# Last phase of a one-core encoder layer: where z's sigmoid is written, when gates are opened and rows finished, and the order of the last unit

## The chip, the cores and the metric

The kernel runs as one program on one core of a Trainium2 chip. The metric is the device time of one execution in microseconds, the median of several runs. The profile is of one execution, taken by the hardware profiler. Engines are named as in the profile: PE (matmul), PEld (weight load), DVE (vector), ACT (scalar, activations), POOL (GpSimd) and SP (the queue from which nearly all DMAs are issued, in order).

## The reference

One layer over 2048 prompt rows (16 tiles of 128) and 8 running streams of 16 rows each (one tile of 128, "the sample", tile number NT = 16). After an adaLN norm, `h @ w_in` gives for each row the q, k, v and z of two branches and the merge gates ga and gb. Both attentions run, the sample's also over caches of 512 past positions. What the last phase computes is:

```python
oa = rms_norm(oa, subln_g) * (1.0 - lam_init)
ya = (oa.reshape(b, s, WIDTH_A) * jax.nn.silu(za)) @ w_branch_a
yb = (ob.reshape(b, s, WIDTH_B) * jax.nn.silu(zb)) @ w_branch_b
out = (jax.nn.sigmoid(ga) * ya + jax.nn.sigmoid(gb) * yb) @ w_out
xp = xp + gate * out            # then y = rms_norm(xp, final_g)
```

All inputs and outputs are float32. The kernel splits each float32 operand of a large matmul into two float16 parts and adds three products.

## The kernel before

**Units.** The projection and the attention go by units: 8 units, each one head (A, even units) or one pair of heads (B, odd units). `steps` lists (unit, tile); within a unit the sample's tile NT stands first, then tiles 0 to 15. For each step the projection (`project`, L423 for q, k, v and z, L495 for a share of the merge gates) is cut into pieces, and all pieces of all steps stand in one list, `line`. The transposes of a step's q and k (`transpose_qk`) stand in the line after piece 5 of the next step. The main loop (L1330) runs over n: for each step it takes from the line up to a target that is paced by the estimated durations and runs LEAD = 5 steps ahead, and interleaves these pieces with the scores of step n and the products of weights and values (`pv`, L706 and L707) of step n - 2. When the line is empty, `early_work` fills the remaining steps evenly: the last branch weight, `first` of tiles 0 and 1 (their inputs), and four branch pieces and a transpose of tile 0. z, o and the gates go through DRAM (z_d, o_d, g_d), the sample's q, k and v through s_d.

**Last phase.** It goes over `tiles` = 0 to 14, the sample, 15, in steps n of its own. For each tile:

- `inputs` loads o (L1218, into hs[0]), z (L1219, into hs[1]) and the gates (L1223, four buffers, two a tile). It takes z's sigmoid into a PSUM bank of tag `mm`, of which there are two, shared with the branch matmuls. POOL multiplies o by z (L1230), DVE multiplies by the sigmoid (four L1236 for half 0, one L1232 for half 1). Then ACT takes the gates' sigmoids in place, then the sum of squares of o, and ACT and DVE (L287, L292) split o into u16, which lies in hs[2].
- `turned` transposes u16 by DMA (L1251).
- `branches`: 48 matmuls in four groups (L1262), each times a gate on DVE (L1264); POOL adds the two branches (L1266); `finish` sums squares (L274), scales and splits the result into y16.
- `turned_y` transposes it by DMA (L1287) into the only buffer of y^T.
- `output`: 48 matmuls (L1399) in two halves, times gate and scale (L1403), plus x on POOL (L1407). Then the row's sum of squares, its rsqrt on DVE (`rsqrt_one`, L255 to L266), the scaling (L1412) and the store (L1413). x has two buffers (L1392).

In step n the branches of tile n run, the output of tile n - 1 and the inputs of tile n + 2. Beside them runs the sample's attention over the caches in pieces (`sample`): cache loads (L758), key transposes (L777) copied out by DVE or ACT (L778), scores (L794), sigmoids or exponentials on ACT, a scan on DVE (L607), transposes of the weights (L812, L818), products (L830).

**Order.** A planner at build time gives each engine its order, by program order and by when its model says that operands are there; on the chip every engine runs its own list in order. Activations that need a table (sigmoid, exponential) go through a helper that keeps them in program order:

```python
def act(**kw):
    i = S.activation(**kw)
    if last_table[0] is not None:
        tc.add_manual_dep(i.ins, last_table[0].ins.name, NOSYNC, reason="table order")
    last_table[0] = i
    return i
```

Their line in the profile is L120, whatever they work on.

Of the kernel before, what the change touches and what calls it, by code (L numbers as in the profile page):

```python
# [16 lines left out]
F32 = mybir.dt.float32  # L17
# [3 lines left out]
AF = mybir.ActivationFunctionType  # L21
ALU = mybir.AluOpType
# [3 lines left out]
P = 128  # L26
D = 1024
# [5 lines left out]
NT = SEQ // P  # L33
# [77 lines left out]
def layer_kernel(ctx: ExitStack, tc: tile.TileContext, a: dict):  # L111
    nc = tc.nc
    V, S, G, T = nc.vector, nc.scalar, nc.gpsimd, nc.tensor
# [4 lines left out]
# [7 lines that stand above are left out]
# [30 lines left out]
    def y_rows(t):  # L155
        return y_p[t * P : (t + 1) * P, :] if t < NT else y_s
# [30 lines left out]
    def bank(tag, dt=F32):  # L187
        return ps.tile([P, 512 if dt == F32 else 1024], dt, tag=tag, name=f"ps_{tag}", bufs=BANKS[tag])
# [113 lines left out]
    units = [None] * 8  # L302
# [200 lines left out]
    def transpose_qk(U, t):  # L503
        g, i = t // 4, t % 4
        q16, k16 = U.pop(("q16", t)), U.pop(("k16", t))
        pt = bank("t", F16)
        for c in range(2):
            T.transpose(pt[:, c * P : (c + 1) * P], k16[:, c, :, :].rearrange("p f d -> p (f d)"), id16)
        for f in range(2):
            for c in range(2):  # L510
                j = 2 + f * 2 + c
                T.transpose(pt[:, j * P : (j + 1) * P], q16[:, f, c, :, :].rearrange("p r d -> p (r d)"), id16)
        if i == 0:
            U["k"][g] = kvp.tile([P, 2, 512], F16, tag="k", name="k", bufs=K_BUFS)
        U["q", t] = qst = stg.tile([P, 4, P], F16, tag="qst", name="qst", bufs=Q_BUFS)
        kst = U["k"][g][:, :, i * P : (i + 1) * P]
        copy = V.tensor_copy if U["kind"] == 1 else S.copy
        (V.tensor_copy if U["u"] == 0 else copy)(out=kst, in_=pt[:, 0:256].rearrange("p (c n) -> p c n", c=2))
        copy(out=qst, in_=pt[:, 256:768].rearrange("p (j n) -> p j n", j=4))
# [343 lines left out]

        return [lambda x=x: one(*x) for x in srcs]

    steps = [(u, t) for u in range(8) for t in [NT] + list(range(NT))]
    back = []
    spare = norms()
    jobs, done = [], []
# [1 line left out]

    line = []

    def begin(u, t):
        if t == NT:
            if u > 0:
                free.extend(units[u - 1]["bufs"])
            finish_unit(u)

    def projection(m):  # L880
        u, t = steps[m]
        made = []

        def piece(i):
            if i == 0:
                begin(u, t)
                made.extend(project(units[u], t))
            if i == H_AT and not at_hand and m + 1 < len(steps) and steps[m + 1] not in ahead:
                fetch_h(*steps[m + 1])
            made[i]()  # L890

        return [lambda i=i: piece(i) for i in range(12 + 3 * GATES[u][1] // 128)]

    starts = []
    for m in range(len(steps)):
        starts.append(len(line))
        for i, fn in enumerate(projection(m)):
            line.append((m, fn))
            if i == TR_AFTER and m > 0 and steps[m - 1][1] < NT:
                line.append((m - 1, lambda m=m: transpose_qk(units[steps[m - 1][0]], steps[m - 1][1])))  # L900
    line.append((len(steps) - 1, lambda: transpose_qk(units[7], NT - 1)))
    starts.append(len(line))
    at = [0]

# [310 lines left out]
    def inputs(t):  # L1215

        o, z = hs[0:2]
        load(out=o, in_=o_d[t])  # L1218
        load(out=z, in_=z_d[t])  # L1219
        gs = []  # L1220
        for j in range(2):
            gs.append(L["g"][(2 * len(begun) + j) % 4].rearrange("p (b n) -> p b n", b=2))
            load(out=gs[j], in_=g_d[t].rearrange("p (b n) -> p b n", b=2)[:, :, j * 512 : (j + 1) * 512])  # L1223
        begun.append(t)
        r = L["orms"][:, 4 * t : 4 * t + 4] if t < NT else rsqrt(osums[:, NT, :], 4, P, tiny, "rA")
        for n in range(2):
            c = slice(n * 512, (n + 1) * 512)
            sg = bank("mm")
            act(out=sg, in_=z[:, c], func=AF.Sigmoid)
            G.tensor_tensor(out=o[:, c], in0=o[:, c], in1=z[:, c], op=ALU.mult)  # L1230
            if n == 1:
                V.tensor_tensor(out=o[:, c], in0=o[:, c], in1=sg, op=ALU.mult)  # L1232
            else:
                for h in range(4):
                    c = slice(h * P, (h + 1) * P)
                    V.scalar_tensor_tensor(out=o[:, c], in0=sg[:, c], scalar=r[:, h : h + 1], in1=o[:, c], op0=ALU.mult, op1=ALU.mult)  # L1236
        for g in gs:
            act(out=g, in_=g, func=AF.Sigmoid)
        acc = tiny.tile([P, 1], F32, tag="uacc", name="uacc")
        sum_squares(o, D, acc)  # L1240
        su = scales(acc, unit, "su")
        u16 = hs[2].bitcast(F16).rearrange("p (f n) -> p f n", f=2)
        split(u16[:, 0, :], u16[:, 1, :], o, su[:, 0:1], S)
        iu = unit.tile([P, 1], F32, tag="iu", name="iu")
        V.tensor_tensor(out=iu, in0=su[:, 1:2], in1=L["s"][0][:, 1:2], op=ALU.mult)
        return dict(u16=u16, u=L["u"][len(begun) % 2], iu=iu, g=gs)

    def turned(st):

# [56 lines left out]
    def early_work():  # L1306


        free.extend(units[7]["bufs"])

        def first(t):
            if "orms" not in L:
                L["orms"] = rsqrt(osums[:, 0:NT, :].rearrange("p t h -> p (t h)"), 4 * NT, P, con, "orms")
            states[t] = inputs(t)
            if t == tiles[0]:
                turned(states[t])

        def early(i):

            if i == 0:  # L1320
                L["first"] = [fn for _, fn in branches(states[tiles[0]])] + [lambda: turned_y(states[tiles[0]])]
            L["first"][i]()

        def rest():
            L["g"], L["u"], (L["y"], L["y16"]) = free[0:4], free[4:6], free[6:8]

        return [branch_weight for _ in branch_weights] + [rest] + [lambda t=t: first(t) for t in tiles[0:2]] \
            + [lambda i=i: early(i) for i in range(5)]
# [31 lines left out]
    with ExitStack() as c2:  # L1360
# [17 lines left out]
        def gate_rows(i, n):  # L1378
# [4 lines left out]
            T.matmul(pg, sel[0:9, i * P : (i + 1) * P], gsm[0:9, :], start=True, stop=True)  # L1383
            return pg

        def output(t, st):
            box = {}

            def half(j):
                if j == 0:  # L1390
                    box["x"] = s2.tile([P, D], F32, tag="x", name="x2", bufs=2)
                    load(out=box["x"], in_=x_rows(t))  # L1392
                x = box["x"]
                c = slice(j * 512, (j + 1) * 512)
                po = bank("o")
                n = 0
                for yi, wi in ((0, 0), (0, 1), (1, 0)):
                    for k in range(KT):
                        T.matmul(po, st["y"][:, yi * 8 + k, :], wo[j * 4 + k // 2][:, wi, k % 2, :], start=(n == 0), stop=(n == 3 * KT - 1))  # L1399
                        n += 1  # L1400
                m = s2.tile([P, 512], F32, tag="sg", name="m", bufs=2)
                if t < NT:
                    V.scalar_tensor_tensor(out=m, in0=po, scalar=st["iy"], in1=gate[:, c], op0=ALU.mult, op1=ALU.mult)  # L1403
                else:
                    S.activation(out=m, in_=po, func=AF.Identity, scale=st["iy"])
                    V.tensor_tensor(out=m, in0=m, in1=gate_rows(1, j), op=ALU.mult)
                G.tensor_tensor(out=x[:, c], in0=m, in1=x[:, c], op=ALU.add)  # L1407
                if j == 1:
                    acc = tiny.tile([P, 1], F32, tag="facc", name="facc")
                    sum_squares(x, D, acc)  # L1410
                    r = rsqrt_one(acc, D, tiny, "rF")
                    V.scalar_tensor_tensor(out=x, in0=x, scalar=r, in1=fg, op0=ALU.mult, op1=ALU.mult)  # L1412
                    load(out=y_rows(t), in_=x)  # L1413

            return [(5.2, lambda j=j: half(j)) for j in range(2)]

# [22 lines left out]
        for n in range(NT + 2):  # L1439
            work = []  # L1440
            if 0 < n <= NT:
                work += branches(states[tiles[n]])
            if n + 1 <= NT:

                work.insert(2, (0.9, lambda n=n: turned(states[tiles[n + 1]])))
            if n + 2 <= NT:
                work.insert(5, (0.1, lambda n=n: states.update({tiles[n + 2]: inputs(tiles[n + 2])})))
            if n > 0:
                work += output(tiles[n - 1], states.pop(tiles[n - 1]))
            if 0 < n <= NT:  # L1450
                work.append((0.9, lambda n=n: turned_y(states[tiles[n]])))
            interleave(work, aside(n))


# [25 lines left out]
```

## Time and profile before

| | |
|---|---|
| median of 3 runs | 2286.06 us (2282.44 to 2286.41) |
| the profiled execution | 2285.48 us, span 2283.7 us |
| busy, PE / PEld / DVE / ACT / POOL | 91% / 49% / 71% / 65% / 30% of the span |
| mean granted PE clock | 0.966 |
| DMA | 411.92 MB, mean 180 GB/s |

Busy time is the time in which an engine executes something. PE's matmuls are pipelined and their ends are modelled, so two that overlap count once. "A <- B" in the lists of waits says that A's engine stood idle until B was done. L numbers are lines of the kernel; a helper's line stands for every caller, and then the names of the tiles tell them apart (`wa<-g_d`: buffer wa, loaded from g_d). The buffers wa and wb are shared by weights, gates, u and y, and keep their names.

### The profile page before, as it was taken

To read this page: it belongs to the slowest core of one execution; us is meant where nothing else is said; L and a number is where in the kernel's file an instruction comes from. 1 tells how busy PE (TensorE), PEld (TensorE's weight loads), DVE (VectorE), ACT (ScalarE), POOL (GpSimd) and SP (SyncE) were. 2 spreads that over 40 slices of the span, in tenths; PEclk is the share of its full clock that TensorE was granted. 3 is DMA by queue.
4 is the path that set the end of the run, shared out by engine and by line. 5 is a ranking of instruction groups with operands and counts; after the bars stand their busy time and mean duration, and the time that the engine had idled before them with its cause. 6 is when DMAs were issued, how large, how long until landed. Compare 5 with 4: busy or idle time off the path is not lost. (4 is left out here: it accounts for less than half of the span.)

```text
span 2283.7 us, 40470 instructions
## 1 busy us (share of the span) xinstructions
PE 2085.1 (91%) x14478; PEld 1110.4 (49%) x14478; DVE 1611.5 (71%) x3507; ACT 1482.6 (65%) x2952; POOL 688.1 (30%) x559
## 2 busy tenths in 40 slices
PE   4997999999999999899999989999986799888997
PEld 2554554555555455455545555555543444444443
DVE  4668767789875778987577898776777656565554
ACT  3877677787876777786677777666776544444431
POOL 1522012355301335530032553012344232232321
PEclk7999999999999999999999999999997899999998
DMA  8667658697875778876566886757687989788652
GB/s 295 211 212 187 163 131 220 148 221 155 206 169 124 170 154 199 177 179 131 128 172 142 204 183 154 153 140 163 151 179 173 295 228 262 202 220 211 188 150 65
DMA packets 763754, 411.92 MB, mean 180 GB/s; under 512 B 524986, under 2 KB 708586, under 8 KB 763040
## 3 DMA queue, kind: packets, MB, share of 16 engines
q1 hardware_dynamic: 762474, 408.86, 72.6%
q8 instruction: 113, 1.85, 0.3%
q14 instruction: 89, 0.73, 0.1%
q10 hardware_dynamic: 1078, 0.48, 0.1%
HBM read 211.53 MB, written 72.91 MB: 125 GB/s over the span
## 5 line engine op out<-in xcount | busy, mean ns | idle before, releaser
L423 PE MATMUL ps_mm<-wb,hs 128*128 128x512 f16 x1836 | 460.7, 382 | 0.6 <-DVE v L292 0.5
L629 POOL TENSOR_TENSOR sc_p<-sc_p,sc_n 128x1024 f32<-128x1024 f32 (+8 forms) x160 | 278.1, 1742 | 459.2 <-DVE sc_n L607 451.6
L423 PEld LDWEIGHTS <-hs 128*128 128x128 f16 x2928 | 256.1, 98 | 226.9 <-issue 6.8
L607 DVE TENSOR_TENSOR_SCAN sc_n<-ps_s,sc_n,zero_t 128x512 f32<-128x512 f32 x192 | 245.3, 1278 | 64.4 <-ACT ps_s L120 62.2
L423 PE MATMUL ps_mm<-wa,hs 128*128 128x512 f16 x1092 | 279.4, 380 | 0.0
L647 PE MATMUL ps_s<-k,qst 128*128 128x512 f16 (+3 forms) x640 | 225.9, 354 | 38.3 <-DVE sc_n L607 30.1
L120 ACT ACTIVATE sc_p<-ps_s,usc 128x512 f32<-128x512 f32 (+3 forms) x320 | 202.0, 631 | 85.8 <-PE ps_s L648 55.1
L495 PE MATMUL ps_mm<-wa,hs 128*128 128x512 f16 x1020 | 257.0, 379 | 0.0
L562 DVE TENSOR_TENSOR sc_n<-sc_p,sc_n 128x1024 f16<-128x1024 f32 (+7 forms) x160 | 197.9, 1242 | 41.3 <-ACT sc_n L561 41.2
L648 PE MATMUL ps_s<-k,qst 128*128 128x512 f16 (+3 forms) x640 | 226.2, 354 | 0.0
L1399 PE MATMUL ps_o<-wo,wb 128*128 128x512 f16 x816 | 199.5, 401 | 24.7 <-DMA wb<-wa 22.0
L706 PE MATMUL ps_o<-v,wt 128*128 128x128 f16 x1008 | 175.6, 226 | 27.6 <-DMA wt<-sc_n 27.5
L495 PEld LDWEIGHTS <-hs 128*128 128x128 f16 x1632 | 140.2, 98 | 119.0
L120 ACT ACTIVATE ps_s<-ps_s,usc 128x512 f32<-128x512 f32 (+3 forms) x320 | 193.7, 605 | 0.0
L561 ACT CAST sc_n<-sc_p 128x1024 f16<-128x1024 f32 (+7 forms) x160 | 138.5, 870 | 49.2 <-POOL sc_p L629 49.1
L707 PE MATMUL ps_o<-v,wt 128*128 128x64 f16 x1008 | 158.5, 198 | 0.0
L495 PE MATMUL ps_mm<-wb,hs 128*128 128x512 f16 x612 | 155.9, 379 | 0.0
L706 PEld LDWEIGHTS <-wt 128*128 128x128 f16 x1008 | 99.2, 102 | 102.7 <-DMA wt<-sc_n 38.0
L1399 PEld LDWEIGHTS <-wb 128*128 128x128 f16 x816 | 82.1, 102 | 130.4 <-DMA wb<-wa 26.1
L457 POOL TENSOR_TENSOR rot<-pr,rope 128x256 f32<-128x256 f32 x68 | 63.1, 928 | 247.1 <-ACT pr L437 193.3
L437 ACT ACTIVATE pr<-ps_mm,usc 128x512 f32<-128x512 f32 (+1 forms) x136 | 86.5, 636 | 67.4 <-PE ps_mm L423 67.1
L545 DVE TENSOR_SCALAR_CACHE_REDUCE sc_n<-ps_s,usc 128x512 f32<-128x512 f32 (+3 forms) x148 | 99.0, 669 | 42.4 <-PE ps_s L648 28.2
(336 smaller groups left out, 4346.7 us busy)
## 6 DMA issues: line engine op xcount, KB each, us to landing
hs<-hT_d SPq DMA_DIRECT2D x122, 512.0 KB, 4.2
g_d<-gt SPq DMA_DIRECT2D x68, 256.0 KB, 3.4
out_dram<-pr SPq DMA_DIRECT2D x204, 64.0 KB, 1.8
wa<-g_d SPq DMA_DIRECT2D x25, 512.0 KB, 6.7
wide<-in_w_ada_dram SPq DMA_DIRECT2D x12, 1024.0 KB, 8.4
wa<-in_w_in_dram SPq DMA_DIRECT2D x44, 256.0 KB, 4.7
z_d<-pr SPq DMA_DIRECT2D x136, 64.0 KB, 2.7
o_d<-o SPq DMA_DIRECT2D x136, 64.0 KB, 2.7
```

The costliest lines, as they stand in the source:

```text
L120: i = S.activation(**kw)
L423: T.matmul(box["p"], box["h"][:, hi, k, :], U["w"][k][:, wi, :], start=(n == 0), stop=(n == 3 * KT - 1))
L495: T.matmul(box["g"][:, 0:gw], box["h"][:, hi, k, :], U["wg"][k // per][:, k % per, wi, :], start=(j == 0), stop=(j == 3 * KT - 1))
L561: S.copy(out=hi, in_=src)
L562: V.tensor_tensor(out=lo, in0=src, in1=hi, op=ALU.subtract)
L607: V.tensor_tensor_scan(out=dst[:, lo : lo + n][:, ::-1], data0=src[:, 0:n][:, ::-1], data1=zero_t[:, 0:1].to_broadcast([P, n]), initial=fi ...
L629: G.tensor_tensor(out=p[:, 0:m], in0=p[:, 0:m], in1=n[:, 1 : m + 1], op=ALU.mult)
L647: T.matmul(p[:, 0:n], qst[:, c, :], kk[:, c, 0:n], start=True, stop=False)
L648: T.matmul(p[:, 0:n], qst[:, 2 + c, :], kk[:, c, 0:n], start=False, stop=not diag)
L706: T.matmul(po[:, c * P : (c + 1) * P], wt[:, wj, :], vt[:, c, :, :], start=first, stop=False)
L707: T.matmul(po[:, c * P : c * P + 64], wt[:, nb + wj, :], vt[:, c, 0, :], start=False, stop=last)
L1399: T.matmul(po, st["y"][:, yi * 8 + k, :], wo[j * 4 + k // 2][:, wi, k % 2, :], start=(n == 0), stop=(n == 3 * KT - 1))
```

## The change

There are four parts, all in the last unit and the last phase.

1. z's sigmoid is written into hs[2], u's buffer, and read from there by L1236 and L1232. Before, it went to a PSUM bank.
2. The gates' sigmoids leave `inputs` for a function of their own, `opened`. In the last phase it is called one step after the loads; for tiles 0 and 1 it still follows their inputs.
3. The end of a row (sum of squares, rsqrt, scaling, store) leaves `output`: the row is put on the list `late`, and `finished` works it off in the next step, after that step's first two branch groups and the transpose of u. One call after the loop does the last row.
4. In unit 7 the sample's tile stands last in `steps`. `begin` looks whether the unit has been begun, in place of asking for tile NT, and the extra transposes after the end of the line go away, since the sample's pieces now follow tile 15.

```diff
-    steps = [(u, t) for u in range(8) for t in [NT] + list(range(NT))]
+    steps = [(u, t) for u in range(7) for t in [NT] + list(range(NT))] + [(7, t) for t in range(NT + 1)]
...
-    def begin(u, t):
-        if t == NT:
+    def begin(u):
+        if "sc" not in units[u]:
...
-    line.append((len(steps) - 1, lambda: transpose_qk(units[7], NT - 1)))
...
-            sg = bank("mm")
+            sg = hs[2][:, c]
             act(out=sg, in_=z[:, c], func=AF.Sigmoid)
...
-                    V.scalar_tensor_tensor(out=o[:, c], in0=sg[:, c], scalar=r[:, h : h + 1], in1=o[:, c], op0=ALU.mult, op1=ALU.mult)
-        for g in gs:
-            act(out=g, in_=g, func=AF.Sigmoid)
+                    V.scalar_tensor_tensor(out=o[:, c], in0=hs[2][:, c], scalar=r[:, h : h + 1], in1=o[:, c], op0=ALU.mult, op1=ALU.mult)
...
+    def opened(st):
+
+        for g in st["g"]:
+            act(out=g, in_=g, func=AF.Sigmoid)
...
             states[t] = inputs(t)
+            opened(states[t])
...
+        late = []
+
+        def finished():
+
+            while late:
+                x, t = late.pop(0)
+                acc = tiny.tile([P, 1], F32, tag="facc", name="facc")
+                sum_squares(x, D, acc)
+                r = rsqrt_one(acc, D, tiny, "rF")
+                V.scalar_tensor_tensor(out=x, in0=x, scalar=r, in1=fg, op0=ALU.mult, op1=ALU.mult)
+                load(out=y_rows(t), in_=x)
...
                 if j == 1:
-                    acc = tiny.tile([P, 1], F32, tag="facc", name="facc")
-                    sum_squares(x, D, acc)
-                    r = rsqrt_one(acc, D, tiny, "rF")
-                    V.scalar_tensor_tensor(out=x, in0=x, scalar=r, in1=fg, op0=ALU.mult, op1=ALU.mult)
-                    load(out=y_rows(t), in_=x)
+                    late.append((x, t))
...
                 work.insert(5, (0.1, lambda n=n: states.update({tiles[n + 2]: inputs(tiles[n + 2])})))
+                if n > 0:
+                    work.insert(6, (0.1, lambda n=n: opened(states[tiles[n + 1]])))
+            elif n + 1 <= NT:
+                work.insert(4, (0.1, lambda n=n: opened(states[tiles[n + 1]])))
+            work.insert(3, (0.1, finished))
...
+        finished()
```

More of the change, by code (lines that the diff above doesn't have):

```diff
@@ L885, in piece @@
             if i == 0:
-                begin(u, t)
+                begin(u)
                 made.extend(project(units[u], t))
```

## The prediction

> **What bounds the kernel now.** I read the busy time by stretches first, because the diff touches only the end of the attention and the last phase. Columns: stretch, length, then busy time (and instructions) of PE, PEld, DVE, ACT and POOL, granted clock, DMA share, GB/s. Below it are the last projection matmuls (L495), the last product of weights and values (L707), the first output matmul (L1399), and one branch group of 24 matmuls from the chain of waits.
>
> ```profile
> span 2283.7 us, 40470 instructions
> ...
> 1600.00:1690.00 90.00, 89.89 (x622) 47.29 (x620) 65.50 (x100) 65.71 (x126) 28.88 (x21) 1.00 0.65 153
> 1690.00:1764.00 74.00, 44.85 (x359) 25.91 (x358) 60.90 (x78) 50.71 (x80) 36.84 (x20) 0.75 0.86 185
> ...
> 1760.00:2080.00 320.00, 284.61 (x2080) 149.34 (x2079) 187.44 (x486) 144.76 (x268) 92.70 (x71) 0.94 0.90 241
> 2080.00:2284.00 204.00, 172.79 (x976) 79.91 (x974) 104.32 (x288) 67.18 (x124) 54.61 (x42) 0.94 0.53 142
> ...
> L495 PE MATMUL ps_mm<-wb,hs x612: 376/379/381, 640.4 to 1687.5; 128*128 128x512 f16 x153
> ...
> L707 PE MATMUL ps_o<-v,wt x1008: 191/193/261, 351.1 to 1763.1; 128*128 128x64 f16 x168
> ...
> L1399 PE MATMUL ps_o<-wo,wb x816: 376/379/635, 1790.6 to 2272.8; 128*128 128x512 f16 x164
> ...
> 2241.38 5.18 PE ps_mm L1262 x24
> ```
>
> Until 1690 PE is full (89.89 of 90 us): there PE's own work is the time. From the last projection (1687.5) to 1763 DVE leads (60.90 of 74) and PE starves. In the last phase PE leads, with the DMA engines close behind until 2080 (0.90). A matmul takes a slot of 5.18/24 = 0.216 us. So what the change can win there is PE's waiting. Next, then, who waits for whom from 1750 to the end: what waits, for what, total us, times, longest; PE, ACT, DVE and the load queue (SPq).
>
> ```profile
> PE ps_o L1399 <- DMA wb<-wa: 22.0, 9, 6.1
> PE ps_t L818 <- DVE dks L778: 9.7, 2, 4.9
> PE ps_s L777 <- DVE dsc L607: 6.8, 3, 2.9
> ...
> PE ps_mm L1262 <- DVE wa L1264: 2.9, 3, 2.1
> ...
> PE ps_t L763 <- DVE rF L266: 2.2, 1, 2.2
> ...
> PE ps_mm L1262 <- DVE r L256: 0.6, 1, 0.6
> ...
> ACT wa L120 <- DMA wa<-g_d: 51.6, 21, 7.0
> ...
> ACT wb L120 <- DMA wb<-g_d: 32.6, 8, 10.0
> ...
> DVE r L255 <- ACT junk L274: 40.1, 13, 5.9
> DVE dsc L607 <- ACT ps_s L120: 27.5, 6, 11.5
> ...
> SPq L1413 <- DVE x L1412: 65.2, 11, 18.5
> SPq L1392 <- DMA out_dram<-x: 36.7, 13, 6.2
> ...
> SPq L1287 <- PE ps_mm L1262: 21.1, 7, 5.7
> ```
>
> ACT stands 51.6 + 32.6 = 84.2 us with a gate's sigmoid at its head whose load has not landed. DVE stands 40.1 us with a row's rsqrt at its head. SP stands 65.2 us with a row's store at its head, and 36.7 us more because the next x load wants that store's buffer. PE itself shows far less: 9.7, 6.8, 2.9, 2.2, 0.6, and 22.0 for the transpose of y. I therefore price each part by the PE waits that it can reach, not by the idle time of the other engines.
>
> **Part 1, gates opened a step later.** No instruction is added or removed: two sigmoids a tile change their place on ACT. The functions that go through `act` keep program order, so a sample's sigmoids queue behind the gates'. The chain of waits at one such place:
>
> ```profile
> 2032.53 5.32 DMA wa<-g_d
> ...
> 2037.93 1.06 ACT wa L120
> ...
> 2039.32 0.51 ACT dsc L120
> 2039.84 0.50 ACT ps_s L120
> ...
> 2040.36 1.29 DVE dsc L607
> ...
> 2041.70 0.66 PE ps_s L777 x4
> ```
>
> Load, gate, the sample's sigmoids, DVE's scan, and only then PE's next transposes (L777). A step later the load has long landed, and the wait is gone. What PE gets is the L777 row: 6.8 us. I take -7. Bounds: 0 if the next thing is late anyway, and -16 if all three places return the 5.32 us of this load (3 x 5.32). Late next is PE's own matmul stream.
>
> **Part 2, z's sigmoid in u's buffer.** Two ACTIVATEs of 512 columns a tile write SBUF instead of two `mm` banks; the four L1236 and one L1232 on DVE read it there. The trace at one of the two long L818 waits, by POOL, ACT, DVE, PE:
>
> ```profile
> 2087.12 2.50 POOL L1230 TENSOR_TENSOR hs<-hs,hs 128x512 f32<-128x512 f32 x2 [12.04 <-DMA hs<-o_d]
> ...
> 2092.91 0.60 ACT L120 ACTIVATE ps_mm<-hs 128x512 f32<-128x512 f32 x1
> ...
> 2093.60 1.13 DVE L1236 SCALAR_TENSOR_TENSOR hs<-ps_mm,orms,hs 128x128 f32<-128x128 f32 x4 [8.03 <-ACT ps_mm L120]
> ...
> 2096.79 0.68 DVE L778 COPY dks<-ps_t 128x512 f32<-128x512 f32 x1
> ...
> 2097.52 0.47 PE L818 MATMUL ps_t<-ident,dsc 128*128 128x128 f32 x1 [4.90 <-DVE dks L778]
> ```
>
> DVE idles 8.03 us at L1236, the copy L778 that PE wants is behind it, and the sigmoid comes last although z was there. With u's buffer free (the transpose L1251 of the tile before has read it) the sigmoid no longer waits for a bank, and L1236 can start when POOL's product is done: 2087.12 + 2.50 = 2089.62 in place of 2093.60, 4.0 us. Twice that is -8; the bank waits (2.9 us) I leave out, since PE must wait for L1264 with two banks anyway. Bounds: 0 (the sigmoid keeps its late place on ACT) and -12.6 (9.7 + 2.9).
>
> What it adds are reads: L1236 and L1232 now have both inputs in SBUF. No row shows them so. The nearest is L562, which has two SBUF inputs, without and with a POOL instruction beside it:
>
> ```profile
> 1717.89 1.08 DVE L562 TENSOR_TENSOR sc_n<-sc_p,sc_n 128x896 f16<-128x896 f32 x1
> ...
> 1725.13 2.34 DVE L562 TENSOR_TENSOR sc_n<-sc_p,sc_n 128x896 f16<-128x896 f32 x1
> ...
> 1724.53 2.00 POOL L629 TENSOR_TENSOR sc_p<-sc_p,sc_n 128x1024 f32<-128x1024 f32 x1 [3.94 <-DVE sc_n L607]
> ```
>
> The second started inside POOL's 2.00 us and took 1.26 us more. One such meeting for each of 17 tiles is 17 x 1.26 = 21.4 us of DVE, not of PE: DVE is busy 104 to 187 us of these stretches, so idle time covers it, and I take 0. Bounds: 0 to +21.4. The Trainium skill, page "SBUF — State Buffer", section "SBUF: two separate sides", speaks against this edit: a DVE instruction with two SBUF inputs and a GpSimd one that reads SBUF lock a shared port pair for a whole instruction each, and the other blocks. The two L562 rows agree. By the page, with every meeting on the path, the sum below would end at 2289.
>
> **Part 3, rows finished a step later.** Square sum, rsqrt chain (ten small DVE instructions), scaling and store of a row move one step on. The squares are then ready when DVE comes to them, and SP meets the store when its row is done. PE's rows that name this chain are 2.2 (L266) and 0.6 (L256): -3. The 22.0 us for y's transpose (L1287) I leave: it waits for y^T's only buffer and for PE (21.1 us in SP's row). Bounds: 0 to -22. An x buffer is held a step longer; its load still comes a step ahead of the add that needs it. The last row's chain stays after the last matmul (2272.8), so the tail keeps its length.
>
> **Part 4, sample projected last in unit 7.** 48 matmuls (10.4 us of PE), two evictions on ACT, and on SP one load and six stores go from the head of the unit to the end of its line. But the line is paced: its last piece still falls at tile 13, where PE is full, so no PE work enters the starved stretch. Working through the loop by hand, the early work of the last phase moves half a step back against the attention: `first(0)` from tile 14 to tile 15, the four branch pieces from beside the last two products to the last and behind. That takes ACT and DVE work off tile 14 (a gain of some us) and may put 10.4 us of branch matmuls behind 1763. PE is free until the first L1399 at 1790.6, which covers 10.4 us. I take 0, bounds -4 to +10.4. SP's six stores fall among the transposes, where two more than before cost little.
>
> **Sum.** -7 - 8 - 3 + 0 = -18 us. The profiled execution took 2285.48 us (span 2283.7 and 1.8 around it), 0.6 below the median 2286.06. 2285.5 - 18 = 2267.5, so 2268.
>
> **Rivals.**
> - *More comes back.* The waits for y^T shrink too, as SP no longer stands behind row stores (65.2 + 36.7 us). Half of 22.0 more, and the bounds of parts 1 and 2: -16 - 12.6 - 3 - 11 = -43, 2243. Against it: SP's own row for L1287 names PE. At half of this extra, 2255.
> - *DMA is the bound.* At 0.90 until 2080, the loads may only move forward into a full queue: 2284, no change. Against it: 0.90 leaves 32 us of 320, and the share falls to 0.53 afterwards.
> - *Port.* Part 2's meetings on the path: 2267.5 + 21.4 = 2289, no change. Against it: DVE's idle time.
> - *A wait takes the place of the one removed (slower).* The sigmoid of z now waits for L1251, and what lies behind it on ACT is the second square sum of y, on which y^T and L1399 hang:
>
> ```profile
> 2162.21 4.05 SPq L1251 DMA_TRANSPOSE wb<-hs  x1
> ...
> 2176.30 0.63 ACT L274 ACTIVATE junk<-wa 128x512 f16<-128x512 f32 x1 [7.84 <-POOL wa L1266]
> ...
> 2176.93 0.58 ACT L120 ACTIVATE ps_mm<-hs 128x512 f32<-128x512 f32 x1
> ...
> DMA to landing us min/median/max: 4.3/6.8/8.5
> ```
>
> The last row is L1251's time to landing. Here it lands near 2169, 8 us ahead of the sigmoid: room. If the planner, seeing no bank in the way, puts the sigmoid right behind the split of u, ACT stands up to 6.8 us for each of 15 tiles, with y's sums behind. From 18/15 = 1.2 us a tile on y's path this decides; at 2 us it is 30 - 18 = +12: 2298.
>
> **How the numbers follow.** Forecast (2256 to 2279, with part 4's 10.4 at its upper end) 0.52, more 0.14, DMA 0.12, port 0.04, slower 0.18. A measurement of this kernel can tell about 0.2% (4.6 us) from no change, that is outside 2281.5 to 2290.6. Faster 0.52 + 0.14 = 0.66, same 0.16, slower 0.18. The range 2250 to 2293 leaves out the far parts of "more" (0.07) and of "slower" (0.11), under 0.2.
>
> **What would show it.** ACT's wait for g_d near zero, DVE's at L255 and SP's at L1413 mostly gone; L1236 starting right after POOL's L1230; the L818 and L777 waits of PE gone, L1399's near 22; attention's end within 5 us of 1763. Wrong if ACT waits for L1251 instead, if L1399's first start moves beyond 1800, or if the four L1236 grow from 1.13 us.

## The result and the profile after

The changed kernel takes 2297.62 us (median, 2293.24 to 2303.49), the kernel before 2286.41 us beside it. The ratio is 1.0052, with a 95% interval of 1.0038 to 1.0065: 11 to 12 us slower, where 18 us faster were forecast, and 4.6 us above the upper end of the range. The profiled execution took 2300.52 us.

Lines move a little: in the changed kernel the u transpose is L1253, the branch matmul L1264, POOL's product of o and z L1229, the four 128-column products L1235, the y transpose L1289, the output matmul L1414, the row's scaling and store L1398 and L1399.

First the busy time by stretches, in the columns of before.

```profile
1690.00:1764.00 74.00, 48.05 (x374) 26.97 (x372) 63.27 (x76) 52.85 (x84) 35.85 (x18) 0.75 0.80 168
1760.00:2080.00 320.00, 273.87 (x1912) 141.88 (x1910) 203.50 (x468) 140.91 (x264) 93.16 (x72) 0.91 0.87 231
2080.00:2299.00 219.00, 190.23 (x1140) 88.21 (x1139) 120.85 (x309) 71.92 (x132) 56.10 (x44) 0.95 0.59 152
```

Then the first and last start of the last projection, of the products of weights and values, and of the output matmuls (behind the colon the shortest, median and longest, in ns):

```profile
L495 PE MATMUL ps_mm<-wb,hs x612: 376/379/380, 642.4 to 1694.7; 128*128 128x512 f16 x153
L707 PE MATMUL ps_o<-v,wt x1008: 191/193/261, 353.9 to 1776.7; 128*128 128x64 f16 x168
L1414 PE MATMUL ps_o<-wo,wb x816: 376/379/634, 1787.7 to 2287.7; 128*128 128x512 f16 x164
```

Between 1760 and 2080 PE did 1912 matmuls and transposes, where the kernel before did 2080, and makes up for nearly all of these 168 after 2080, with 1140 where there were 976. The attention ends at 1776.7 in place of 1763.1; 7.2 us of this are there at its last projection matmul (1694.7 in place of 1687.5). So PE falls behind at the end of the attention and in the first steps of the last phase, and is not slower afterwards: the output of the sixth tile starts 18.5 us later than before, and the span ends 14.9 us later.

The waits from 1750 to the end:

```profile
PE ps_o L1414 <- DMA wb<-wa: 14.2, 9, 3.3
PE ps_mm L1264 <- DVE wb L1266: 7.5, 3, 6.0
PE ps_mm L1264 <- DVE r L255: 6.3, 2, 3.5
...
PE ps_mm L1264 <- DMA wb<-hs: 5.7, 2, 4.2
...
PE ps_mm L1264 <- DMA wa<-hs: 5.0, 1, 5.0
PE ps_t L818 <- DVE dks L778: 2.9, 3, 1.4
...
PE ps_s L777 <- DVE dsc L607: 2.4, 1, 2.4
...
ACT hs L120 <- DMA wb<-hs: 24.9, 5, 6.8
...
ACT hs L120 <- DMA wa<-hs: 17.7, 4, 6.1
...
DVE r L255 <- ACT junk L274: 29.2, 9, 7.4
...
SPq L1399 <- DVE x L1398: 60.1, 8, 18.3
```

The waits that the prediction wanted gone are smaller: L818 2.9 us (9.7 before), L777 2.4 (6.8), and ACT's for the gates 4.9 (84.2). New is a wait of z's sigmoid for the transpose of u (`ACT hs L120 <- DMA ...<-hs`, 24.9 + 17.7 us), and of the branch matmuls for u's transpose (5.7 + 5.0 us). The first would be the prediction's slower rival. Whether it is, and where, the experiments tell.

For all runs the table gives the ratio to the kernel before, and two lengths read from the profiled execution: the **tail**, from the last L495 matmul to the last L707, and the **last phase**, from there to the end of the span. The start of the tail itself lies anywhere between 1687.5 and 1697.9 in the profiles of kernels that have the same code up to unit 7, so the lengths are to be compared, not the clock times, and differences of a few us are decided by the ratio.

Two things limit the lengths. Two pairs of kernels have, on every engine, the same operations on the same tiles in the same order, as far as the names and shapes in the traces tell: parts 1, 3 and part 1 alone; tiles 0 and 1 in banks and DVE after POOL. Within a pair the lengths differ by up to 4.7 us and the ratios by up to 0.0007, so that much is noise. And part 4 moves the start of the tail: the last 154 projection matmuls (L423 and L495) stretch over 47.2 us in all five kernels with it and over 44.0 in all others. So 3.2 us of a shorter tail with part 4 are no gain.

| kernel | median us | ratio (95%) | tail | last phase |
|---|---|---|---|---|
| before | 2285 to 2287 | 1 | 75.6 | 520.6 |
| the change, parts 1 to 4 | 2297.62 | 1.0052 (1.0038 to 1.0065) | 82.0 | 521.9 |
| part 4 alone | 2292.76 | 1.0040 (1.0026 to 1.0053) | 70.1 | 528.8 |
| parts 1, 2, 3 | 2301.53 | 1.0074 (1.0055 to 1.0094) | 88.7 | 522.1 |
| part 2 alone | 2306.25 | 1.0092 (1.0076 to 1.0107) | 88.2 | 528.8 |
| parts 1, 3 | 2280.47 | 0.9989 (0.9976 to 1.0001) | 75.9 | 512.4 |
| part 2, tiles 0 and 1 in banks | 2285.58 | 1.0003 (0.9992 to 1.0014) | 72.2 | 520.5 |
| part 2, half in an own buffer | 2287.96 | 1.0011 (1.0000 to 1.0022) | 73.4 | 520.5 |
| part 2, DVE after POOL | 2288.80 | 1.0010 (1.0000 to 1.0020) | 76.9 | 519.4 |
| part 1 alone | 2283.47 | 0.9990 (0.9980 to 1.0001) | 74.0 | 516.8 |
| part 2, tile 1 in banks | 2287.87 | 1.0014 (1.0004 to 1.0025) | 74.3 | 518.3 |
| **all parts, tiles 0 and 1 in banks** | 2277.87 | 0.9967 (0.9956 to 0.9979) | 70.4 | 511.7 |
| parts 1, 2, 3, tiles 0 and 1 in banks | 2282.61 | 0.9986 (0.9975 to 0.9996) | 74.5 | 515.4 |
| parts 1, 3, 4 | 2279.58 | 0.9972 (0.9962 to 0.9981) | 69.2 | 514.7 |
| part 2, tile 1 in y's buffer | 2280.99 | 0.9974 (0.9964 to 0.9984) | 73.9 | 515.7 |
| part 2, tile 1's inputs last | 2288.82 | 1.0015 (1.0003 to 1.0028) | 70.7 | 526.1 |
| all parts, tile 1 in y's buffer | 2281.71 | 0.9984 (0.9972 to 0.9995) | 70.6 | 514.3 |
| parts 1, 2, 3, tile 1 in y's buffer | 2286.21 | 1.0009 (0.9996 to 1.0023) | 73.4 | 519.9 |

### The profile page after: what moved, and what is told of

Same layout as the page of the kernel before. It is cut to its first block, busy times and chain, and to the rows that moved or that the text cites. A ratio compares the mean times of both kernels' runs of the same rounds, so it can differ in the third digit from the quotient of the medians.

```text
span 2298.6 us, 40437 instructions
## 1 busy us (share of the span) xinstructions
PE 2092.3 (91%) x14478; PEld 1112.3 (48%) x14478; DVE 1642.6 (71%) x3507; ACT 1482.1 (64%) x2952; POOL 692.4 (30%) x559
## 5 line engine op out<-in xcount | busy, mean ns | idle before, releaser
L423 PE MATMUL ps_mm<-wb,hs 128*128 128x512 f16 x1836 | 460.0, 381 | 1.7 <-ACT gt L498 1.0
L423 PEld LDWEIGHTS <-hs 128*128 128x128 f16 x2928 | 256.2, 98 | 226.0 <-issue 7.0
L423 PE MATMUL ps_mm<-wa,hs 128*128 128x512 f16 x1092 | 279.3, 380 | 0.0
L495 PE MATMUL ps_mm<-wa,hs 128*128 128x512 f16 x1020 | 256.7, 379 | 0.0
L120 ACT ACTIVATE sc_p<-ps_s,usc 128x512 f32<-128x512 f32 (+3 forms) x320 | 201.8, 631 | 70.3 <-PE ps_s L648 44.6
L562 DVE TENSOR_TENSOR sc_n<-sc_p,sc_n 128x1024 f16<-128x1024 f32 (+7 forms) x160 | 196.7, 1234 | 48.9 <-ACT sc_n L561 48.6
L1414 PE MATMUL ps_o<-wo,wb 128*128 128x512 f16 x816 | 195.9, 393 | 20.1 <-DMA wb<-wa 14.2
L495 PEld LDWEIGHTS <-hs 128*128 128x128 f16 x1632 | 139.7, 98 | 117.6
L120 ACT ACTIVATE ps_s<-ps_s,usc 128x512 f32<-128x512 f32 (+3 forms) x320 | 193.6, 605 | 0.0
L707 PE MATMUL ps_o<-v,wt 128*128 128x64 f16 x1008 | 159.2, 198 | 0.0
L495 PE MATMUL ps_mm<-wb,hs 128*128 128x512 f16 x612 | 156.4, 379 | 0.0
L706 PEld LDWEIGHTS <-wt 128*128 128x128 f16 x1008 | 99.3, 102 | 105.0 <-DMA wt<-sc_n 40.0
L1414 PEld LDWEIGHTS <-wb 128*128 128x128 f16 x816 | 80.6, 101 | 121.6 <-issue 20.3
L437 ACT ACTIVATE pr<-ps_mm,usc 128x512 f32<-128x512 f32 (+1 forms) x136 | 86.6, 637 | 65.2 <-PE ps_mm L423 63.0
L707 PEld LDWEIGHTS <-wt 128*128 128x128 f16 x1008 | 97.5, 101 | 63.8 <-issue 0.8
```

Of the source, the lines that this page charges most:

```text
L423: T.matmul(box["p"], box["h"][:, hi, k, :], U["w"][k][:, wi, :], start=(n == 0), stop=(n == 3 * KT - 1))
L495: T.matmul(box["g"][:, 0:gw], box["h"][:, hi, k, :], U["wg"][k // per][:, k % per, wi, :], start=(j == 0), stop=(j == 3 * KT - 1))
L562: V.tensor_tensor(out=lo, in0=src, in1=hi, op=ALU.subtract)
L706: T.matmul(po[:, c * P : (c + 1) * P], wt[:, wj, :], vt[:, c, :, :], start=first, stop=False)
L707: T.matmul(po[:, c * P : c * P + 64], wt[:, nb + wj, :], vt[:, c, 0, :], start=False, stop=last)
```

## The experiments

**Which part costs.** Three theories for these four: A, part 2's buffer and part 4's place cost only together; B, part 4's order alone costs; C, part 2's buffer alone costs, in either order of unit 7.

Part 4 alone (the hunks of `steps`, `begin` and the extra transposes):

```diff
-    steps = [(u, t) for u in range(8) for t in [NT] + list(range(NT))]
+    steps = [(u, t) for u in range(7) for t in [NT] + list(range(NT))] + [(7, t) for t in range(NT + 1)]
...
```

> Part 4 alone (the sample last in unit 7); parts 1 to 3 as before. Theory A (meeting): the +11 us come at the attention's end, where tile 1's early sigmoid of z waits for the transpose of tile 0's u and tile 15's last score sigmoids stand behind it in table order. It needs part 2's buffer and part 4's place together: here z's sigmoid goes to a bank, so 2286 to 2290, attention's end (last L707) within 5 us of 1763. Theory B (order): the early work's later place costs by itself: 2295 to 2299, last L707 near 1774. Theory C (buffer alone): 2286.

Measured: +7.7 us, ratio 1.0040. Parts 1 to 3, without that hunk:

> Parts 1 to 3 without part 4. Theory A: tile 1's early inputs stand beside the first half of tile 15, few score sigmoids behind them are late: 2282 to 2288, last L707 within 5 us of 1763. Theory B: 2284 to 2287. Theory C: the wait for the transpose costs in any order: 2295 to 2299, last L707 near 1774. If the last phase itself gives back 18 us as the prediction had it: 2268.

Measured: ratio 1.0074, slower than the whole change. Part 2 alone:

```diff
-            sg = bank("mm")
+            sg = hs[2][:, c]
...
-                    V.scalar_tensor_tensor(out=o[:, c], in0=sg[:, c], ...
+                    V.scalar_tensor_tensor(out=o[:, c], in0=hs[2][:, c], ...
```

> Part 2 alone (z's sigmoid in u's buffer). Theory A: 2283 to 2290; in the last phase the L818 waits of PE fall from 9.7 us, as in the changed kernel (2.9). Theory B: 2284 to 2287. Theory C: 2295 to 2299 with the last L707 near 1774. The prediction's part 2 alone: 2278.

Measured: +21.2 us, ratio 1.0092, the slowest of all. Parts 1 and 3 (`opened` and `finished`, z's sigmoid in the banks, old order):

> Parts 1 and 3 (gates opened and rows finished a step later), z's sigmoid in a bank, the old unit order. All three theories: attention's end within 3 us of 1763. The prediction's parts 1 and 3: -10, 2276. If what the other engines no longer wait for is only replaced by other waits, as PE's sum of waits in the changed kernel says: 2284 to 2289.

Measured: ratio 0.9989, with an interval that ends at 1.0001. The medians differ by 4.6 us, the ratio says 2.5, hardly to be told from none. So A falls as the only cause. C holds, though both kernels lose more than it said (2301.53 and 2306.25 against 2299 at most). Part 4 costs by itself as well, but not where B put it: its attention ends at 1764.3, not near 1774. The loss of part 2 is 12.6 us of tail and 8.2 us of last phase. That led to the next question.

**Where in part 2.** Two theories for the last phase: P, the products that read both operands from SBUF stretch beside POOL; W, z's sigmoid waits for u's transpose. In the first kernel tiles 0 and 1, whose inputs are made in the tail by `early_work`, keep the banks (`L["late"]` is set at the start of the last phase):

```diff
-            sg = hs[2][:, c]
+            sg = hs[2][:, c] if "late" in L else bank("mm")
...
```

> Part 2 alone, but for the two tiles whose inputs are made under the attention's last steps (0 and 1), which keep the PSUM banks. Two theories of what part 2 costs in the last phase: P, the four 128-column products (L1236) that now read both large operands from SBUF stretch beside POOL's work (344 to 771 ns mean there); W, z's sigmoid waits for the u transpose that still reads its buffer, with the rest of ACT behind it. Both say that the tail's loss (+11 us in the kernel with part 2 alone) came from the two early tiles: attention's end back within 3 us of before, last phase still +8, time 2295 (2290 to 2299), against 2306 with all of part 2. If the tail's loss has another cause: 2303 to 2308.

Measured: 2285.58 us, ratio 1.0003. Both theories said that 8 us of last phase would stay. Nothing stays: the last phase is 520.5 us, as before. So part 2's loss comes from the two early tiles, and in the last phase part 2 neither costs nor brings anything that the measurement can tell (-1.8 to +3.2 us).

P can be read off this run by itself. The groups of the four products, first of the kernel before, then of this one:

```profile
L1236 DVE SCALAR_TENSOR_TENSOR hs<-ps_mm,orms,hs 128x128 f32<-128x128 f32 x64 | 18.1, 343 | 33.7 <-ACT ps_mm L120 21.0 <-POOL hs L1230 8.7 <-issue 4.0
```

```profile
L1236 DVE SCALAR_TENSOR_TENSOR hs<-hs,orms,hs 128x128 f32<-128x128 f32 x56 | 41.2, 793 | 21.4 <-POOL hs L1230 20.8 <-ACT hs L120 0.7
L1236 DVE SCALAR_TENSOR_TENSOR hs<-ps_mm,orms,hs 128x128 f32<-128x128 f32 x8 | 2.2, 338 | 0.0
```

The stretch is there (mean duration of one product 793 against 343 ns; over all 68 products 50.5 us against 23.3), and the time is that of before. P falls: these 27 us of DVE were covered.

The next kernel takes the wait away in the last phase and keeps the SBUF read:

```diff
-            sg = bank("mm")
+            sg = L["zs"] if "zs" in L and n == 0 else bank("mm")
...
```

> No wait for the u transpose: the first half of z's sigmoid, the one that the four 128-column products read, goes to an SBUF buffer of its own in the last phase; its second half and the two early tiles keep the PSUM banks (the row selector is loaded in two halves to make room). P: the products still stretch, mean 650 to 800 ns there, time 2291 to 2297 (+6 to +10). W: nothing is lost any more, time 2283 to 2288, whatever the products take.

Measured: ratio 1.0011, products 690 ns in the mean. The time lies in W's forecast and the products stretch as P says, so it is against P; but by the run before it there was no loss left in the last phase to divide. The one after it:

```diff
...
+        V.tensor_tensor(out=o[:, 512:1024], in0=o[:, 512:1024], in1=sgs[1], op=ALU.mult)
+        for h in range(4):
...
```

> As the kernel with the early tiles in banks (sigmoid in u's buffer in the last phase), but VectorE's products come after both of POOL's products of the tile, the 512-column one first. P: the 128-column products are back near 345 to 450 ns in the mean and the loss mostly gone, time 2284 to 2290. W: the sigmoids wait for the transpose as before, time 2293 to 2298.

Measured: ratio 1.0010, products 743 ns in the mean. The time lies in P's forecast, but the edit did not reach the chip: on every engine the trace has the same operations on the same tiles in the same order as with the early tiles in banks, since the planner orders the work again. So this is a second measurement of that kernel (1.0003 the first time), and it tells nothing of P. The last of this group was part 1 alone, the gates' sigmoids in `opened`:

> Part 1 alone (gates opened a step behind their loads). The prediction gave it -7 and part 3 -3, the two together measured -4.6. By those terms' proportion part 1 alone gives -3 (2282, 2279 to 2284), with ACT's waits for g_d gone. Rival: the gain of the two is the rows' alone, and this is 2284 to 2288.

Measured: -2.3 us, ratio 0.9990 (the interval ends at 1.0001). In size as expected, hardly to be told from none. And the order of every engine is the same as in the kernel with parts 1 and 3: the planner places the end of a row alike with and without part 3. So part 3 on top of part 1 changes nothing, the rival falls, and 0.9989 and 0.9990 are two measurements of part 1.

**Which early tile.** Tile 0 finds hs[2] free. Tile 1 finds tile 0's u in it.

```diff
-            sg = hs[2][:, c]
+            sg = bank("mm") if len(begun) == 2 else hs[2][:, c]
...
```

> Part 2 alone, with only tile 1, the second of the two early tiles, back in the PSUM banks. Theory W1 (the loss is made where tile 1's z sigmoid has to wait for the transpose of tile 0's u out of the same buffer, with the last score sigmoids behind it in the fixed order of ACT's table work): tile 0 finds the buffer free, so the loss is gone here as with both tiles in banks, 2283 to 2288. Rival O (any change of the early tiles' buffer makes the planner place their work otherwise, and the place is what costs): 2293 to 2306.

Measured: 2287.87 us, ratio 1.0014: 18 of the 21 us are gone with tile 1 alone. Three kernels beside it tried the combinations:

> The whole change, but for the two early tiles, which keep the PSUM banks. W1: the change (+11) loses its tail, and parts 1 and 3 are left with what part 4 costs: 2281 to 2288. If part 2's loss lay in the last phase too when the gates come later, or part 4 costs its +7.7 here: 2289 to 2296.

Measured: 2277.87 us, ratio 0.9967. This is the whole change but for the place of the two early tiles' sigmoids, and it is faster than before by 5 to 10 us, and faster than W1 had it.

> Parts 1 and 3, and part 2 in the last phase alone (early tiles in banks, unit 7 in its old order). Part 2 without the early tiles measured 0 and parts 1 and 3 -4.6: 2281, 2277 to 2284, the best of the candidates. If u's buffer binds once the gates' sigmoids come later (z's sigmoid waits for the transpose, which is then the older work on ACT): 2285 to 2292.

Measured: 2282.61 us, ratio 0.9986. In the range, but not the best: part 2 in the last phase adds nothing to parts 1 and 3.

> Parts 1, 3 and 4, z's sigmoid in the banks as before. If part 4's cost alone (+7.7) is a loss of its own, 2286 to 2291; if it came from where the first tiles' work fell in that one order, as its place between the outputs of the first and third tile says, and parts 1 and 3 move that work, it is within 3 us of parts 1 and 3 alone: 2278 to 2284.

Measured: 2279.58 us, ratio 0.9972. Part 4 costs nothing here, and beside the whole change with early tiles in banks (0.9967) part 2 again is worth nothing in the last phase.

**Wait or slow products.** Tile 1 back in a bank takes away both the wait and the SBUF reads. The next two separate them. First, tile 1's sigmoid in SBUF, in the buffer of y^T, which is idle then:

```diff
-            sg = hs[2][:, c]
+            sg = (L["y"] if len(begun) == 2 else hs[2])[:, c]
...
```

> Part 2 alone, tile 1's z sigmoid in the SBUF buffer that later takes y's transpose and is idle then. W1 (the wait for tile 0's transpose is the cause): the wait is gone and the SBUF reads stay, so the time is that with tile 1 in banks, 2284 to 2291. Rival S (products with both operands in SBUF cost it in the attention's tail, where VectorE is busiest): 2300 to 2307, as with all of part 2.

Measured: 2280.99 us, ratio 0.9974. S falls and W1 holds: the same part 2, with the same SBUF reads, goes from +21 to -6 us when tile 1 need not wait for the transpose. It is 3 us below W1's range; the gain was not foreseen.

How the wait costs so much is seen in the times of a few instructions of the tail. All rows have start, duration, engine, line. The kernel before: z's sigmoids of tile 1, the first of the last score sigmoids, the last scan, PE's next weight product, DVE's products of tile 1, PE's first branch matmul of tile 0, and the y transpose of tile 1.

```profile
1726.09 1.16 ACT L120 ACTIVATE ps_mm<-hs 128x512 f32<-128x512 f32 x2
...
1729.03 0.72 ACT L120 ACTIVATE sc_p<-ps_s,usc 128x512 f32<-128x512 f32 x1
...
1744.50 1.27 DVE L607 TENSOR_TENSOR_SCAN sc_n<-ps_s,sc_n,zero_t 128x512 f32<-128x512 f32 x1
...
1747.03 0.29 PE L706 MATMUL ps_o<-v,wt 128*128 128x128 f16 x1 [5.63 <-DMA wt<-sc_n]
...
1748.09 1.11 DVE L1236 SCALAR_TENSOR_TENSOR hs<-ps_mm,orms,hs 128x128 f32<-128x128 f32 x4
...
1749.35 1.01 PE L1262 MATMUL ps_mm<-wa,wb 128*128 128x512 f16 x2 [0.86 <-DVE hs L1236]
...
1815.53 3.14 SPq L1287 DMA_TRANSPOSE wb<-wa  x1
```

Part 2 alone:

```profile
1735.45 1.99 SPq L1251 DMA_TRANSPOSE wb<-hs  x1
...
1738.90 0.37 ACT L688 ACTIVATE ob<-ps_o,usc 128x128 f32<-128x128 f32 x1 [5.82 <-PE ps_o L707]
1739.89 1.15 ACT L120 ACTIVATE hs<-hs 128x512 f32<-128x512 f32 x2 [0.62 <-DMA wb<-hs]
...
1742.84 0.67 ACT L120 ACTIVATE sc_p<-ps_s,usc 128x512 f32<-128x512 f32 x1
...
1757.83 2.66 DVE L607 TENSOR_TENSOR_SCAN sc_n<-ps_s,sc_n,zero_t 128x512 f32<-128x512 f32 x2
...
1837.94 4.39 SPq L1287 DMA_TRANSPOSE wb<-wa  x1
```

z's sigmoids of tile 1 go from 1726.09 to 1739.89, 13.8 us later: they may only write when the transpose issued at 1735.45 has read u. The attention's score sigmoids stand behind them in the fixed order of `act`, and go from 1729.03 to 1742.84, the same 13.8 us. The last scan follows (1744.50 to 1757.83 and the one after), and the last weight product (1763.1 to 1776.0). Tile 1's y transpose is 22.4 us later, and the span ends 21.1 us later. Between the two the distance is not constant (the output of tile 2 starts 7.8 us later, those from tile 4 on about 20), and how the 13 us of the tail become 21 was not followed. The row with the wait itself shows only 0.62 us, because ACT's order by then had an eviction (L688, 5.82 us of waiting for PE) ahead of the sigmoid: this row of the waits does not show the price of the edit.

Tile 1 in y's buffer, the kernel with -6 us:

```profile
1726.18 1.27 ACT L120 ACTIVATE wb<-hs 128x512 f32<-128x512 f32 x2
...
1729.12 0.80 ACT L120 ACTIVATE sc_p<-ps_s,usc 128x512 f32<-128x512 f32 x1
...
1742.69 1.03 PE L1262 MATMUL ps_mm<-wa,wb 128*128 128x512 f16 x2 [0.88 <-DMA wb<-hs]
...
1744.92 1.27 DVE L607 TENSOR_TENSOR_SCAN sc_n<-ps_s,sc_n,zero_t 128x512 f32<-128x512 f32 x1
...
1747.49 3.88 DVE L1236 SCALAR_TENSOR_TENSOR hs<-wb,orms,hs 128x128 f32<-128x128 f32 x4
```

The sigmoids are back in place. And PE starts tile 0's branches at 1742.69, in the 5.63 us in which it waited for a transpose of weights before; in the kernel before, these matmuls wait until 1749.3, since tile 1's sigmoids, done at 1727, hold the two banks until its products have read them (1748.09 and 1.11). So with tile 1 out of the banks PE works where it stood before. The four products take 3.88 us instead of 1.11, and the kernel is still the faster one. Against the kernel with tile 1 in banks (1.0014; there these matmuls start at 1749.74) tile 1's buffer is the only difference, and it is worth 0.0040, about 9 us. That the early start alone makes this gain is not shown: with parts 1, 2 and 3 and the same buffer the matmuls start at 1742.70 too, and the kernel is no faster than before (1.0009).

In the whole change the same wait stands at the same place, only with two pairs of score sigmoids behind it, since part 4 shifts the tail's work:

```profile
1745.17 1.84 SPq L1253 DMA_TRANSPOSE wb<-hs  x1
...
1749.60 1.15 ACT L120 ACTIVATE hs<-hs 128x512 f32<-128x512 f32 x2 [4.46 <-DMA wb<-hs]
...
1752.55 0.67 ACT L120 ACTIVATE sc_p<-ps_s,usc 128x512 f32<-128x512 f32 x1
```

The second way to take the wait away keeps u's buffer and moves tile 1's inputs to the end of `early_work`:

```diff
...
-        return [branch_weight for _ in branch_weights] + [rest] + [lambda t=t: first(t) for t in tiles[0:2]] \
-            + [lambda i=i: early(i) for i in range(5)]
+        return [branch_weight for _ in branch_weights] + [rest] + [lambda: first(tiles[0])] \
+            + [lambda i=i: early(i) for i in range(5)] + [lambda: first(tiles[1])]
```

> Part 2 alone in u's buffer for all tiles, but tile 1's inputs come after all of tile 0's early branch pieces, so that the transpose of tile 0's u is over when its sigmoids are issued, and the last score sigmoids stand ahead of them. W1: most of the 21 us is gone, and what is left is tile 1 starting later: 2285 to 2294. Rival S: the products are as slow as before, and the time stays at 2300 or more.

Measured: ratio 1.0015. The tail is short (70.7 us), the last phase 5.5 us longer than before, since tile 1 starts late. As W1 expected.

**Do the parts add up?**

> The whole change, with tile 1's z sigmoid in y's idle buffer. If the parts add up once the wait is gone: part 2 -5.8 (measured with this buffer), parts 1, 3 and 4 -5.9, together -11.7, 2274 (2271 to 2277). If they fill the same stalls, it is near the whole change with both early tiles in banks (-7.6): 2277 to 2280. If the wait was not all of the change's loss: above 2283.

Measured: 2281.71 us, ratio 0.9984, slower than both forecasts for a change that adds up or overlaps, below the one for a loss with another cause (above 2283), and still faster than before. None of the three was met.

> The same without part 4. Part 4 measured +7.7 alone, but -1.3 on top of parts 1 and 3, and -4.7 on top of these and part 2 in the last phase alone: this should be 2 to 5 us slower than the whole change with that buffer, 2276 to 2282; if part 4 costs +7.7 by itself, it is that much faster instead, below 2272.

Measured: ratio 1.0009. Neither gain is there, though part 2 alone with this buffer has 0.9974 and parts 1 and 3 have 0.9989. The parts do not add, and these runs do not say why. The time, 2286.21 us, is above the forecast range; only the distance was right: this is slower than with part 4, by 4.5 us in the medians and 0.0025 (6 us) in the ratios.

## Why the prediction was wrong, point by point

**Part 2 is the step that failed.** The text put -8, with bounds of 0 and -12.6 for the edit, on the ground that u's buffer is free when z's sigmoid comes, "the transpose L1251 of the tile before has read it". That was checked at places in the last phase. For tile 1 in the attention's tail it is false, and there the work behind the sigmoid on ACT is the attention's own. Measured: +21 alone. The slower rival named the right wait, the right instruction and the right reason, but placed it in the last phase with y's sums behind it, and priced it at 2 us a tile. That its 2298 met the measured 2297.62 is luck: the loss is made by one tile in the tail, not by fifteen tiles of 2 us each. In the last phase the wait exists and no cost of it can be measured. The fastest kernel of the table, by its list of waits from 1750 on, still has

```profile
ACT hs L120 <- DMA wb<-hs: 23.8, 4, 9.2
```

One tile and one place made the loss. What the -8 was worked out from did come: in the kernel with part 2 and the early tiles in banks the wait of L1236 for the sigmoid falls from 21.0 us to 0.7 (the groups above), and the L818 waits from 9.7 us to 0.8. But PE has other waits in their place, and the time is that of before, so in the last phase the term is 0 and not -8:

```profile
PE ps_t L763 <- DVE r L265: 4.8, 1, 4.8
...
PE ps_mm L1262 <- DMA wb<-hs: 3.6, 1, 3.6
PE ps_mm L1262 <- DVE r L265: 3.2, 1, 3.2
```

**Port.** The estimate from the L562 rows was 21.4 us more of DVE; it is 27.2 (50.5 - 23.3) for L1236 alone, and the text was right to count it as 0 on PE. Of the 68 products of the kernel with part 2 alone, the 13 that ran wholly beside a POOL instruction took 1276 ns in the mean, the 39 that met none 340; in the kernel before, with one input in a bank, 342 and 344. This agrees with the Trainium skill, page "SBUF — State Buffer", section "SBUF: two separate sides": when a DVE instruction with two SBUF inputs and a GpSimd one that reads SBUF meet, one holds the shared ports for the whole instruction and the other blocks.

**Part 1** was put at -7 and measured -2.3 alone. ACT's waits for the gates fall from 84.2 us to 10.2, so the wait was rightly found, and pricing it by PE's waits and not by ACT's was right too. But the whole wait at L777 (6.8 us) was counted as the gates'; with part 1 alone it is still 4.2:

```profile
PE ps_s L777 <- DVE dsc L607: 4.2, 2, 2.3
```

The term was mis-sized: most of that wait has another cause than the gates. That the 2.6 us which went are the 2.3 us of gain is not shown, since other waits of PE change as well (L812 for POOL from 1.0 us to 5.4).

**Part 3** was put at -3. On top of part 1 it is 0, for a reason that the text did not think of: it assumed that a later place in the program is a later place on the engine, and the planner gives every engine the same order with and without it. Its signs did not come: with parts 1 and 3 DVE waits 42.5 us at L255 (40.1 before) and SP 55.5 us at the row's store (65.2); in the whole change it is 29.2 and 60.1. Beside parts 2 and 4 it was not taken out.

**Part 4** was put at 0, from -4 to +10.4. Alone it is +7.7, inside. The text expected a gain in the tail; it is there, but of the 5.5 us (75.6 to 70.1) 3.2 are the moved start. It expected PE to be free from 1763 to 1790.6 and to cover the branch matmuls that come later. That reading was wrong: in the kernel before PE is busy for 17.29 of these 27.5 us, with tile 1's branches among others. The cost came in the first tiles of the last phase (528.8 against 520.6). On top of parts 1 and 3 it is a gain in all four pairs, by the difference of the ratios 0.0017, 0.0019, 0.0022 and 0.0025, 4 to 6 us. What parts 1 and 3 take from its cost is open.

**The sum** was a sum of parts measured on one trace. With the wait gone, the best kernel with all four parts is at -7.6 us (0.9967), not -18. The terms are not independent; that the parts share the same stalls would explain it, but is not shown.

## What to carry to other kernels

When a result moves into a buffer that another step drains, look at every caller, the warm-up path first: ask who still reads the buffer at the first use, and what stands behind the waiting instruction in its engine's fixed order. Do not look for the price in the list of waits alone; put the start of the same instructions side by side in both traces, since a delay that is spread by an order may stand in no row of that list. Where a planner orders the instructions, look first whether an edit changes their order at all: two of the edits here did not. And try the parts of a change one by one: here one tile's buffer hid what the rest was worth.

## What the runs showed of the hardware that was not expected

A long stop of PE can cost more than its own length. In the kernel with part 4 alone PE waits 4.90 us for y's transpose, and then runs at half clock. Stretches of that kernel (the first number after the five busy times is the granted clock), and then the row of the stop:

```profile
1897.00:1902.00 5.00, 0.11 (x1) 0.00 (x0) 1.69 (x3) 2.53 (x4) 0.00 (x0) 0.92 1.05 241
1902.00:1908.00 6.00, 5.99 (x15) 2.15 (x16) 0.38 (x2) 0.00 (x0) 1.68 (x2) 0.50 0.95 292
1908.00:1914.00 6.00, 6.00 (x35) 3.48 (x34) 3.53 (x12) 2.31 (x5) 2.07 (x2) 1.00 0.32 98
```

```profile
1902.01 1.46 PE L1398 MATMUL ps_o<-wo,wb 128*128 128x512 f16 x3 [4.90 <-DMA wb<-wa]
```

The 15 matmuls of the 6 us behind the stop would take 15 x 0.216 = 3.2 us at full clock, so 2.8 us are lost beyond the 4.90. By the Trainium skill, page "TensorE: Matmul & The Clock Gate", section "What's actually happening", PE runs at half rate after an idle window until it has been busy for a while. This trace agrees (0.50, then 1.00). A list of waits counts such a stop too low.
